# A decoder trunk with a top-2-of-8 mixture of experts: pairs of weight loads split in smaller pieces, and parts of the first expert's and the plan's work moved

## The chip, the cores and the metric

The kernel runs on one core of one Trainium2 chip. The metric is the device time of one execution in microseconds (us), the median of several runs.

## What is computed

Layer 0 is a recurrent mixer beside cross-attention into 256 memory tokens, then a dense SwiGLU. Layer 1 is differential attention beside memory cross-attention, then a mixture of eight SwiGLU experts of which each of the 256 tokens uses two. Every sub-layer ends in a layer norm. All data are fp32. The change touches the experts and the router ahead of them:

```python
logits = (xt @ w_router).astype(jnp.float32)
top_v, top_e = lax.top_k(logits, TOP_K)
gates = jax.nn.softmax(top_v, axis=-1)
...
def expert_block(args):
    xb, e = args
    gu = xb @ w13[e]
    return (jax.nn.silu(gu[:, :EXPERT_DIM]) * gu[:, EXPERT_DIM:]) @ w2[e]
```

D_MODEL is 1024 and EXPERT_DIM 3584, so the experts' weights are 8 x 3 x 1024 x 3584 fp32 numbers, 352 MB, which are read once.

## The kernel before, in words

**Weights.** Each weight is split on the chip into an upper part (fp32r, a copy by ScalarE, L124 or L130) and a lower part (the weight less its upper part, a subtraction by VectorE, L106 or L131), and TensorE multiplies with both. The class `Stream` (L32 to L148) does this for all weights in one fixed order. A load of 1 MB, 128 x 2048 numbers, goes into a free slot: one of four `raw` tiles or `x_hi`, which come back after the split, or, once each, `h3_hi`, `h3_lo` and four `early` tiles `e0` to `e3` (L1032). A split takes places from `room`: five `part` tiles, `h1` (a tile named `h` in the rows) and `x_lo`, each 128 x 2048. All loads are issued by SP, in order; a load waits in SP's queue until the subtraction that read its slot is done. `take` (L135) first calls `split` as far as places are free and then hands out the next pieces; a place comes back with the last piece that it holds.

A load is split in one of three ways. The first stage's two loads (`whole` false) are split by 1024 columns, each piece with both parts in one place: four small sets. All others (`whole` true) are split whole: upper part in one place, lower part in another, two pieces. For the stages of place 1 (`whole` "pair") two loads are split whole one after the other, and their pieces are interleaved only when both are done, because a block of place 1 uses column halves of both loads in turn.

**Places and stages.** The experts stand in places 0 to 7: place 0 is expert 0, the others follow by number of tokens (`PLACE`, L207). Places 2, 3 and 4 have 128 rows, 0 and 5 to 7 have 64, place 1 has 128 + 8. Each place has 21 stages, `g`, `u` and `w` for each of seven blocks of 512 hidden columns, and each stage uses two loads. `moe_seq` (L241 to L248) writes out the order: seven stages of place 0 (`head`), then places 2 and 0 mixed, place 3, then each stage of place 1 among three of places 7, 6 and 5, then place 4. The `g` and `u` stages of place 1 go to `run_moving` (L1347), where the weights stand still and the tokens move (L1365, L1366). The other stages multiply at L368 to L370 (128 rows) or L1276 and L1277 (64 rows).

**The router.** After the last layer norm's first half the loop at L996 transposes each token tile (L1005, copied by ScalarE at L1006), multiplies with the router (L1008) and keeps TensorE busy with other matmuls (`keep_warm`, 6 and 15). VectorE then picks two experts per token (L1039 to L1068), makes the dispatch matrix of expert 0 (`dispatch`, L1086), and `gather_first` (L1216) collects its tokens with TensorE. During the router `st.hold` keeps `split` from making anything.

**The plan.** What the other places need is made by a generator, `plan` (L1099 to L1179): the order of the experts, ranks, dispatch matrices of all places, gates, counts, the two parts `h3_hi` and `h3_lo` of the tokens, and `y`, the tokens scaled. A second generator, `gather(4, True, blocks[2])`, collects the tokens of place 2. Both stand in `slow`; `beat_` (L1210) takes one step of `slow` after each piece of weights during the first stages. Place 2's first stage waits for its gather.

## Time and profile before

| what | value |
|---|---|
| runs | median 1576.31 us of 3 (1575.55 to 1577.61) |
| profiled execution | 1579.21 us |
| its span | 1577.4 us |
| TensorE matmul busy | 1533.0 us (97%) |
| VectorE busy | 1239.3 us (79%) |
| ScalarE busy | 1055.8 us (67%) |
| GpSimd busy | 31.9 us (2%) |
| moved by DMA | 451.60 MB, 286 GB/s mean |

The span runs from the first to the last instruction of the profiled execution. Engines are PE (TensorE matmul), PEld (its weight load), DVE (VectorE), ACT (ScalarE), POOL (GpSimd) and SP, whose queue (SPq) issues the loads. Busy shares are means over stages with different limits, so the rows below are taken stage by stage. The experts run from about 574 us to the end.

### The profile page before, as it was taken

What the parts mean: (1) busy time and instruction counts of PE and PEld (TensorE: products, weight loads), DVE (VectorE), ACT (ScalarE), POOL (GpSimd) and SP (SyncE); (2) the same over time, 40 slices, a digit from 0 to 9 for tenths busy, and PEclk for the clock granted to TensorE, in tenths of its full rate; (3) what the DMA queues carried; (4) which work ended last, traced back from release to release, by engine and by line L of the source; (5) the groups of instructions that cost most, each with busy time, mean ns of one, the idle gap of its engine ahead of it and who ended that gap; (6) DMA issues with size and microseconds to landing.
All of it is one profiled execution on the core that took longest, in us unless ns stands there. A gap on an engine that the chain in (4) does not pass through costs nothing.

```text
span 1577.4 us, 22581 instructions
## 1 busy us (share of the span) xinstructions
PE 1533.0 (97%) x8697; PEld 1300.5 (82%) x8697; DVE 1239.3 (79%) x1205; ACT 1055.8 (67%) x1142; POOL 31.9 (2%) x60
## 2 busy tenths in 40 slices
PE   8999999999999989999999999999999999999996
PEld 7988999999998857887888888887878787877774
DVE  6678654555757579888999879889899899889876
ACT  5784544444456457877887778778778787877663
POOL 0000000000000111000000000000000000000000
PEclk9999999999999999999999999999999999999998
DMA  9454655555533755999999999999999999999982
GB/s 295 161 187 161 233 183 183 183 182 197 167 128 126 265 206 194 377 377 387 395 389 352 333 324 353 356 377 377 357 339 377 371 373 353 361 371 363 333 307 98
DMA packets 218678, 451.60 MB, mean 286 GB/s; under 512 B 7241, under 2 KB 62610, under 8 KB 218562
## 3 DMA queue, kind: packets, MB, share of 16 engines
q1 hardware_dynamic: 217490, 446.76, 79.2%
q0 software_dynamic: 1072, 3.32, 0.7%
q8 instruction: 70, 1.15, 0.3%
q14 instruction: 46, 0.38, 0.1%
HBM read 449.00 MB, written 1.05 MB: 285 GB/s over the span
## 4 chain that ended last, share of the span: by engine, by line
PE 79%; DVE 10%; ACT 4%; DMA 4%; issue 2%; POOL 0%; POOLq 0%; SPq 0%; DVEq 0%; ACTq 0%
PE mm L368 11%; PE mm L370 11%; PE mm L369 11%; PE acc L369 6%; PE acc L370 6%; PE acc L368 6%; DVE part L106 5%; PE mm L1276 4%; PE mm L1277 4%; PE mm L1365 3%; DMA raw<-in_moe_w 3%; PE acc L1277 3%; PE acc L1276 3%; PE mm L1299 2%; PE mm L1255 1%
## 5 line engine op out<-in xcount | busy, mean ns | idle before, releaser
L124 ACT ACTIVATE part<-raw 128x2048 fp32r<-128x2048 f32 x188 | 359.2, 1914 | 58.9 <-DMA raw<-in_moe_w 21.6
L106 DVE TENSOR_TENSOR part<-raw,part 128x2048 fp32r<-128x2048 f32 x150 | 341.1, 2284 | 16.1 <-PE mm L370 5.5
L131 DVE TENSOR_TENSOR part<-raw,part 128x1024 fp32r<-128x1024 f32 x166 | 201.4, 1223 | 126.2 <-ACT part L130 125.6
L130 ACT ACTIVATE part<-raw 128x1024 fp32r<-128x1024 f32 x166 | 173.1, 1056 | 87.8 <-PE mm L370 47.8
L368 PE MATMUL mm<-x_hi,part 128*128 128x256 f32 x768 | 220.0, 286 | 2.1 <-ACT part L130 2.1
L370 PE MATMUL mm<-x_hi,part 128*128 128x256 f32 x768 | 218.3, 284 | 1.1 <-DVE part L131 1.1
L369 PE MATMUL mm<-x_lo,part 128*128 128x256 f32 x768 | 217.7, 283 | 0.0
L368 PEld LDWEIGHTS mm<-x_hi,part 128*128 128x128 f32 x768 | 147.9, 193 | 5.3 <-ACT part L130 2.6
L370 PEld LDWEIGHTS mm<-x_hi,part 128*128 128x128 f32 x768 | 147.8, 192 | 1.7 <-DVE part L131 1.6
L369 PEld LDWEIGHTS mm<-x_lo,part 128*128 128x128 f32 x768 | 147.8, 192 | 0.7
L1276 PE MATMUL mm<-part,xs 128*128 128x512 f32 x248 | 98.8, 398 | 0.0
L124 ACT ACTIVATE part<-x_hi 128x2048 fp32r<-128x2048 f32 x46 | 88.0, 1914 | 15.2 <-PE mm L1277 4.0
L1277 PE MATMUL mm<-part,xs 128*128 128x512 f32 x248 | 97.9, 395 | 0.0
L368 PE MATMUL mm<-part,xg 128*128 128x512 f32 x240 | 97.1, 404 | 0.0
L369 PE MATMUL mm<-part,xg 128*128 128x512 f32 x240 | 95.2, 397 | 1.8 <-DVE part L106 1.5
L370 PE MATMUL mm<-part,xg 128*128 128x512 f32 x240 | 94.7, 395 | 0.0
L106 DVE TENSOR_TENSOR part<-x_hi,part 128x2048 fp32r<-128x2048 f32 x37 | 84.5, 2285 | 7.5 <-PE mm L1365 2.5
L106 DVE TENSOR_TENSOR x_lo<-raw,h 128x2048 fp32r<-128x2048 f32 x37 | 84.6, 2285 | 5.8 <-PE mm L370 2.8
L106 DVE TENSOR_TENSOR h<-raw,part 128x2048 fp32r<-128x2048 f32 x38 | 86.8, 2284 | 1.6 <-ACT part L124 1.1
L106 DVE TENSOR_TENSOR part<-raw,x_lo 128x2048 fp32r<-128x2048 f32 x37 | 84.5, 2285 | 2.7 <-PE mm L1365 1.1
L124 ACT ACTIVATE x_lo<-raw 128x2048 fp32r<-128x2048 f32 x37 | 70.8, 1914 | 13.9 <-PE mm L1277 5.1
L1365 PE MATMUL mm<-xg,part 128*128 128x272 f32 x320 | 79.6, 335 | 0.0
(513 smaller groups left out, 3489.5 us busy)
## 6 DMA issues: line engine op xcount, KB each, us to landing
raw<-in_moe_w SPq DMA_DIRECT2D x262, 1024.0 KB, 7.3
x_hi<-in_moe_w SPq DMA_DIRECT2D x66, 1024.0 KB, 7.3
raw<-in_ffn_w SPq DMA_DIRECT2D x42, 1024.0 KB, 4.9
raw<-in_a_w_in SPq DMA_DIRECT2D x10, 1024.0 KB, 9.4
raw<-in_mem_w_kv SPq DMA_DIRECT2D x8, 1024.0 KB
raw<-in_w_kv_shared SPq DMA_DIRECT2D x8, 1024.0 KB, 6.1
raw<-in_a_w_out SPq DMA_DIRECT2D x6, 1024.0 KB, 4.8
raw<-in_b_w_q SPq DMA_DIRECT2D x6, 1024.0 KB
```

Of the source, the lines that this page charges most:

```text
L106: nc.vector.tensor_sub(lo, src, hi.bitcast(F32))
L124: nc.scalar.activation(hi, src, AF.Copy)
L130: nc.scalar.activation(hi, src, AF.Copy)
L131: nc.vector.tensor_sub(lo, src, hi.bitcast(F32))
L368: PE.matmul(o, lhsT=l_hi, rhs=r_hi, start=start, stop=False)
L369: PE.matmul(o, lhsT=l_hi, rhs=r_lo, start=False, stop=False)
L370: PE.matmul(o, lhsT=l_lo, rhs=r_hi, start=False, stop=stop)
L1255: PE.matmul(p[:, k], lhsT=src[:, t, f], rhs=disp[:, t, g0:g0 + ng], start=t == 0, stop=t == 1)
L1276: PE.matmul(o[h], lhsT=w[:, kt], rhs=w_hi[:, i, f], start=a, stop=False)
L1277: PE.matmul(o[h], lhsT=w[:, kt], rhs=w_lo[:, i, f], start=False, stop=z)
L1299: PE.matmul(p[:, i], lhsT=src[:, i * 128:(i + 1) * 128], rhs=fold, start=True, stop=True)
L1365: PE.matmul(p[m], lhsT=w_hi[:, k, f], rhs=x_[:, kt], start=a, stop=False)
```

## The change

1. A pair of place 1 is split by 1024 columns: `piece` hands out the first half of the first load, the first of the second, the second of the first and the second of the second, and each takes one place for both parts.
2. The last three of the first stage's four small sets are made during the router: `upper` makes the upper parts between the two token tiles, `lower` the lower parts at three points of VectorE's work.
3. In `plan` the dispatch of place 2 comes first, then the two parts of the tokens, as soon as the loads in those two tiles have been split (`uses(once)`), then the gather of place 2, and only then the dispatches of the other places.

```diff
@@ -42,7 +42,7 @@
 
         self.nc, self.free, self.room = nc, deque(free), deque(room)
         self.todo, self.loaded, self.ready, self.hold = deque(), deque(), deque(), False
-        self.known, self.half, self.pair = False, None, None
+        self.known, self.half, self.turn, self.uppers = False, None, 0, deque()
 
     def add(self, ap, a, b, cols=False, whole=False):
 
@@ -65,7 +65,7 @@
             pool, name, again = slot
             v = pool.tile([128, 2048], F32, name=name)[:, :a * b].rearrange("p (a b) -> p a b", a=a)
             self.nc.sync.dma_start(v, ap() if callable(ap) else ap)
-            self.loaded.append(([v] if whole else self.halves(v, cols), cols, whole, slot))
+            self.loaded.append(([v] if whole is True else self.halves(v, cols), cols, whole, slot))
 
     @staticmethod
     def halves(v, cols):
@@ -85,7 +85,7 @@
     def uses(self, slots):
 
         return any(slot in slots for slot in list(self.free) + [l[3] for l in self.loaded] +
-                   ([self.half[3]] if self.half else []))
+                   ([self.half[3]] if self.half else []) + [u[3] for u in self.uppers])
 
     def tiles(self, place, n, m, parts):
         pool, names, _ = place
@@ -94,41 +94,75 @@
         t = pool.tile([128, 2048], F32R, name=names[0])[:, :parts * n * m]
         return t.rearrange("p (s a b) -> s p a b", s=parts, a=n)
 
+    def piece(self):
+
+        todo, cols, whole, slot = self.loaded[0]
+        if whole == "pair":
+
+            if len(self.loaded) < 2:
+                return None
+            second = self.loaded[1]
+            first, self.turn = self.turn == 0, 1 - self.turn
+            if first:
+                src = todo.pop(0)
+                return src, cols, whole, None if todo else slot
+            src = second[0].pop(0)
+            if second[0]:
+                return src, cols, whole, None
+            self.loaded.popleft()
+            self.loaded.popleft()
+            return src, cols, whole, second[3]
+        src = todo.pop(0)
+        if not todo:
+            self.loaded.popleft()
+        return src, cols, whole, None if todo else slot
+
+    def upper(self):
+
+        src, _, whole, slot = self.piece()
+        assert whole is False
+        place = self.room.popleft()
+        hi, lo = self.tiles(place, *src.shape[1:], 2)
+        self.nc.scalar.activation(hi, src, AF.Copy)
+        self.uppers.append((hi, lo, src, slot, place))
+
+    def lower(self):
+
+        hi, lo, src, slot, place = self.uppers.popleft()
+        self.nc.vector.tensor_sub(lo, src, hi.bitcast(F32))
+        if slot:
+            self.back(slot)
+        self.ready.append((hi, lo, (place,)))
+
     def split(self):
         nc = self.nc
         self.load()
         while self.room and not self.hold and (self.loaded or self.half):
-            place = self.room.popleft()
             if self.half:
-                hi, src, cols, slot, first, whole = self.half
+                hi, src, cols, slot, first = self.half
                 self.half = None
+                place = self.room.popleft()
                 lo = self.tiles(place, *src.shape[1:], 1)[0]
                 nc.vector.tensor_sub(lo, src, hi.bitcast(F32))
                 self.back(slot)
                 pieces = list(zip(self.halves(hi, cols), self.halves(lo, cols)))
-                pieces = [(*w, (first, place) if w is pieces[-1] else ()) for w in pieces]
-                if whole == "pair" and not self.pair:
-                    self.pair = pieces
-                else:
-                    if self.pair:
-                        pieces = [w for two in zip(self.pair, pieces) for w in two]
-                        self.pair = None
-                    self.ready += pieces
+                self.ready += [(*w, (first, place) if w is pieces[-1] else ()) for w in pieces]
             else:
-                todo, cols, whole, slot = self.loaded[0]
-                src = todo.pop(0)
-                if not todo:
-                    self.loaded.popleft()
-                if whole:
+                got = self.piece()
+                if not got:
+                    break
+                src, cols, whole, slot = got
+                place = self.room.popleft()
+                if whole is True:
                     hi = self.tiles(place, *src.shape[1:], 1)[0]
                     nc.scalar.activation(hi, src, AF.Copy)
-                    self.half = hi, src, cols, slot, place, whole
+                    self.half = hi, src, cols, slot, place
                 else:
-                    if not todo:
-                        self.back(slot)
                     hi, lo = self.tiles(place, *src.shape[1:], 2)
                     nc.scalar.activation(hi, src, AF.Copy)
                     nc.vector.tensor_sub(lo, src, hi.bitcast(F32))
+                    if slot:
+                        self.back(slot)
                     self.ready.append((hi, lo, (place,)))
             self.load()
 
@@ -993,7 +1027,8 @@
             ln_tail(*ahead[0], gb, h3[:, 0])
     l1t.close()
     hp = ctx.enter_context(tc.tile_pool(name="hp", bufs=1, side="right"))
-    st.free += [(hp, "h3_hi", False), (hp, "h3_lo", False)]
+    once = [(hp, "h3_hi", False), (hp, "h3_lo", False)]
+    st.free += once
     st.load()
 
     hT = lp.tile([128, 2, KT, 128], F32, name="vd")
@@ -1009,6 +1044,10 @@
         keep_warm((6, 15)[t])
         if t:
             ln_tail(*ahead[1], gb, h3[:, 1])
+            st.lower()
+        else:
+            for _ in range(3):
+                st.upper()
     l1.close()
     catp.close()
     pa.close()
@@ -1065,6 +1104,7 @@
         PE.matmul(ct[:, 16:24], lhsT=ones, rhs=mb[:, t], start=t == 0, stop=t == 1)
     val = S("val", 2, 8)
     DVE.tensor_scalar(val, mb, -BIG, BIG, op0=OP.mult, op1=OP.add)
+    st.lower()
     DVE.tensor_add(val, val, ct[:, :16].rearrange("p (t e) -> p t e", t=2))
     rank = S("rank", 2, 8)
     gate = S("gate", 2, 8)
@@ -1087,6 +1127,7 @@
                               op0=OP.is_equal)
 
     dispatch((0, 0, 64), val)
+    st.lower()
 
     ord_i = mo.tile([1, NE - 1], I32, name="ord_i")
     cs_i = mo.tile([1, NE + 1], I32, name="cs_i")
@@ -1130,12 +1171,22 @@
             POOL.tensor_tensor(tmp[:, t], sel, val[:, t, None, 1:].to_broadcast([128, q, q]), op=OP.mult)
         DVE.tensor_reduce(rank[:, :, 1:], tmp, axis=AX.X, op=OP.add)
         yield
+        dispatch(*PLACE[2])
+        yield
+        while st.uses(once):
+            yield
+        h3_parts.extend(hp.tile([128, 2, D], F32R, name=f"h3_{s}") for s in ("hi", "lo"))
+        hi, lo = h3_parts
+        for t in range(2):
+            ACT.activation(hi[:, t], h3[:, t], AF.Copy)
+            DVE.tensor_sub(lo[:, t], h3[:, t], hi[:, t].bitcast(F32))
+            yield
+        yield from gather(4, True, blocks[2])
         for bs in PLACE.values():
             for b in bs:
-                if b[0]:
+                if b[0] not in (0, 2):
                     dispatch(b)
-            if bs[0][0] % 2:
-                yield
+                    yield
         g1 = S("g1", 2)
         POOL.tensor_scalar(g1, d, 1.0, None, op0=OP.add)
         DVE.reciprocal(g1, g1)
@@ -1168,12 +1219,6 @@
         POOL.tensor_copy(cs_i[:, :NE], cs[0:1])
         POOL.tensor_copy(cs_i[:, NE:], over[0:1])
         yield
-        h3_parts.extend(hp.tile([128, 2, D], F32R, name=f"h3_{s}") for s in ("hi", "lo"))
-        hi, lo = h3_parts
-        for t in range(2):
-            ACT.activation(hi[:, t], h3[:, t], AF.Copy)
-            DVE.tensor_sub(lo[:, t], h3[:, t], hi[:, t].bitcast(F32))
-            yield
         for t in range(2):
             ACT.activation(y[:, t], h3[:, t], AF.Copy, scale=ALPHA)
             yield
@@ -1500,7 +1545,7 @@
         (4, "g", 3): [late_gb],
         (4, "u", NJ - 1): [wait_slow, lambda: setattr(last, "dt", back(last, mt(), F32, "sh", 2))],
     }
-    slow += [plan(), gather(4, True, blocks[2])]
+    slow.append(plan())
     run_experts(moe_seq, blocks, st, hooks)
     wait_slow()
 
```

On VectorE around the router's end (names of tiles as in the rows; `part` and `x_hi`, `x_lo` are the places and slots above), before:

```order
L1067 TENSOR_SCALAR val<-mb 128x16
L1068 TENSOR_TENSOR val<-val,mm 128x16
L1086 TENSOR_SCALAR disp<-slots,val 128x64 x2
L1228 TENSOR_TENSOR ys_5466<-mm,ys_5466 128x2x64 x2
L1228 TENSOR_TENSOR ys_5466<-mm,ys_5466 128x4x64
L131 TENSOR_TENSOR part_5492<-x_hi,part_5492 128x1024
L131 TENSOR_TENSOR part_5497<-x_lo,part_5497 128x1024
L131 TENSOR_TENSOR part_5500<-x_lo,part_5500 128x1024
L106 TENSOR_TENSOR h_5505<-raw_5095,part_5503 128x2048
L106 TENSOR_TENSOR part_5519<-raw_5152,x_lo 128x2048
```

and now:

```order
L465 SCALAR_TENSOR_TENSOR h_5058<-qd,rstd,kd 128x512 x2
L132 TENSOR_TENSOR part_5367<-x_hi,part_5367 128x1024
L1078 SCALAR_TENSOR_TENSOR lg<-mm,rstd,b_rt 128x8 x2
...
L1106 TENSOR_SCALAR val<-mb 128x16
L132 TENSOR_TENSOR part_5369<-x_lo,part_5369 128x1024
L1108 TENSOR_TENSOR val<-val,mm 128x16
L1126 TENSOR_SCALAR disp<-slots,val 128x64 x2
L132 TENSOR_TENSOR part_5371<-x_lo,part_5371 128x1024
L1273 TENSOR_TENSOR ys_5477<-mm,ys_5477 128x2x64 x2
L1273 TENSOR_TENSOR ys_5477<-mm,ys_5477 128x4x64
L146 TENSOR_TENSOR h_5505<-raw_5095,part_5503 128x2048
L146 TENSOR_TENSOR part_5519<-raw_5152,x_lo 128x2048
```

The three subtractions of 128 x 1024 that stood behind the gather's (`ys`) now stand ahead of the router's first step (`lg`), ahead of `val` and behind the dispatch of expert 0.

On VectorE between the ranks and the split of place 2's first set, before (a `disp` row with 128 columns is a whole place, with 64 a place of 64 rows):

```order
L1131 TENSOR_REDUCE rank<-tmp 128x2x7
L1086 TENSOR_SCALAR disp<-slots,rank 128x128 x2
...
L106 TENSOR_TENSOR part_5584<-raw_5234,part_5562 128x2048
L1086 TENSOR_SCALAR disp<-slots,rank 128x64 x6
L106 TENSOR_TENSOR x_lo<-h_hi,h_5588 128x2048
L1086 TENSOR_SCALAR disp<-slots,rank 128x128 x6
L1141 RECIPROCAL g_5632<-g_5632 128x2
L106 TENSOR_TENSOR part_5636<-h_lo,part_5609 128x2048
...
L106 TENSOR_TENSOR part_5775<-x_hi,part_5743 128x2048
L106 TENSOR_TENSOR x_lo<-raw_5507,h_5779 128x2048
L106 TENSOR_TENSOR part_5830<-raw_5555,part_5805 128x2048
L106 TENSOR_TENSOR part_5856<-raw_5560,part_5834 128x2048
```

and now:

```order
L1172 TENSOR_REDUCE rank<-tmp 128x2x7
L1126 TENSOR_SCALAR disp<-slots,rank 128x128 x2
L146 TENSOR_TENSOR part_5578<-raw_5234,part_5562 128x2048
L146 TENSOR_TENSOR x_lo<-h_hi,h_5582 128x2048
L146 TENSOR_TENSOR part_5614<-h_lo,part_5597 128x2048
...
L146 TENSOR_TENSOR x_lo<-raw_5507,h_5765 128x2048
L1126 TENSOR_SCALAR disp<-slots,rank 128x64 x4
L146 TENSOR_TENSOR part_5808<-raw_5555,part_5787 128x2048
L1126 TENSOR_SCALAR disp<-slots,rank 128x64 x2
L1126 TENSOR_SCALAR disp<-slots,rank 128x128 x2
L146 TENSOR_TENSOR part_5826<-raw_5560,part_5812 128x2048
L1126 TENSOR_SCALAR disp<-slots,rank 128x128 x2
```

Of the dispatches only that of place 2 stays ahead of the splits of the first stages; four of 128 columns, two of 64 and the plan's later steps now stand behind the split of place 2's first set (`part_5808<-raw_5555`, before `part_5856<-raw_5560` and `part_5830<-raw_5555`).

On VectorE at the first stage of place 1 (L1372, now L1417, is the stage's first tail), before:

```order
L1435 TENSOR_TENSOR sg<-sg,mm 128x512
L106 TENSOR_TENSOR part_8229<-raw_8082,part_8206 128x2048
L106 TENSOR_TENSOR x_lo<-raw_8120,h_8233 128x2048
L1308 TENSOR_TENSOR hd<-mm,hd 128x512
L106 TENSOR_TENSOR part_8276<-raw_8146,part_8251 128x2048
L1372 TENSOR_TENSOR sg<-sg,mm 128x136 x2
L106 TENSOR_TENSOR part_8337<-x_hi,part_8280 128x2048
L1372 TENSOR_TENSOR sg<-sg,mm 128x136 x2
L106 TENSOR_TENSOR h_8365<-raw_8204,part_8341 128x2048
```

and now:

```order
L163 TENSOR_TENSOR part_8206<-raw_8082,part_8206 128x1024
L1480 TENSOR_TENSOR sg<-sg,mm 128x512
L163 TENSOR_TENSOR part_8230<-raw_8120,part_8230 128x1024
L163 TENSOR_TENSOR h_8233<-raw_8082,h_8233 128x1024
L163 TENSOR_TENSOR x_lo<-raw_8120,x_lo 128x1024
L1353 TENSOR_TENSOR hd<-mm,hd 128x512
L146 TENSOR_TENSOR part_8280<-raw_8146,part_8255 128x2048
L146 TENSOR_TENSOR part_8302<-x_hi,part_8284 128x2048
L1417 TENSOR_TENSOR sg<-sg,mm 128x136 x2
L146 TENSOR_TENSOR h_8347<-raw_8204,part_8329 128x2048
L1417 TENSOR_TENSOR sg<-sg,mm 128x136 x2
```

The pair (`raw_8082` and `raw_8120`) was two whole subtractions and is four small ones in order of use, and at the first tail one more whole set has been split.

On SP the order of the loads changes in one place: the second load into `x_hi` comes ahead of the four into the early tiles instead of behind them.

## Rows read from the trace of the kernel before

**Rows 1.** Busy time by stretch: start:end, length, PE, PEld, DVE, ACT, POOL, clock, DMA share, GB/s
```profile
575.00:622.00 47.00, 38.65 (x172) 29.34 (x173) 43.29 (x56) 39.58 (x40) 10.78 (x25) 0.93 0.48 169
622.00:675.00 53.00, 53.00 (x267) 44.15 (x266) 45.30 (x28) 41.98 (x40) 0.00 (x0) 1.00 1.02 373
957.00:1406.00 449.00, 435.16 (x2444) 365.44 (x2443) 402.55 (x319) 353.29 (x346) 0.64 (x1) 1.00 1.00 364
991.00:995.00 4.00, 4.00 (x22) 3.96 (x22) 3.31 (x3) 2.11 (x3) 0.00 (x0) 0.57 0.90 355
```

**Rows 2.** Timeline of ACT, 561 to 580 us: start, us, instruction, idle before and releaser
```profile
561.90 1.09 ACT L1006 ACTIVATE vd<-mm 128x512 f32<-128x512 f32 x2 [3.30 <-PE mm L1005]
574.28 1.05 ACT L130 ACTIVATE part<-x_hi 128x1024 fp32r<-128x1024 f32 x1
575.23 2.00 ACT L130 ACTIVATE part<-x_lo 128x1024 fp32r<-128x1024 f32 x2
577.13 1.91 ACT L124 ACTIVATE part<-raw 128x2048 fp32r<-128x2048 f32 x1
```

**Rows 3.** Timeline of DVE, 564 to 582 us
```profile
564.54 0.36 DVE L1039 SCALAR_TENSOR_TENSOR lg<-mm,rstd,b_rt 128x8 f32<-128x8 f32 x2 [1.83 <-PE mm L1008]
569.59 0.17 DVE L1068 TENSOR_TENSOR val<-val,mm 128x16 f32<-128x16 f32 x1 [2.00 <-PE mm L1065]
576.51 2.35 DVE L131 TENSOR_TENSOR part<-x_lo,part 128x1024 fp32r<-128x1024 f32 x2
579.07 2.29 DVE L106 TENSOR_TENSOR h<-raw,part 128x2048 fp32r<-128x2048 f32 x1 [0.20 <-ACT part L124]
```

**Rows 4.** The page's costliest groups: busy, mean ns of one, idle before and releaser
```profile
L124 ACT ACTIVATE part<-raw 128x2048 fp32r<-128x2048 f32 x188 | 359.2, 1914 | 58.9 <-DMA raw<-in_moe_w 21.6
L106 DVE TENSOR_TENSOR part<-raw,part 128x2048 fp32r<-128x2048 f32 x150 | 341.1, 2284 | 16.1 <-PE mm L370 5.5
L131 DVE TENSOR_TENSOR part<-raw,part 128x1024 fp32r<-128x1024 f32 x166 | 201.4, 1223 | 126.2 <-ACT part L130 125.6
L130 ACT ACTIVATE part<-raw 128x1024 fp32r<-128x1024 f32 x166 | 173.1, 1056 | 87.8 <-PE mm L370 47.8
```

**Rows 5.** Timeline of SP's queue, 560 to 630 us
```profile
564.58 2.78 SPq L67 DMA_DIRECT2D e<-in_moe_w  x4
615.85 0.37 SPq L67 DMA_DIRECT2D x_hi<-in_moe_w  x1
617.95 7.46 SPq L67 DMA_DIRECT2D raw<-in_moe_w  x4
```

**Rows 6.** Timeline of DVE, 591 to 621 us
```profile
591.75 1.06 DVE L1086 TENSOR_SCALAR disp<-slots,rank 128x64 fp32r<-128x64 f32 x6
594.93 1.25 DVE L1086 TENSOR_SCALAR disp<-slots,rank 128x128 fp32r<-128x128 f32 x6
596.11 0.15 DVE L1141 RECIPROCAL g<-g 128x2 f32<-128x2 f32 x1
605.45 0.16 DVE L1167 TENSOR_SCALAR cs<-cs 128x8 f32<-128x8 f32 x1
617.84 2.28 DVE L106 TENSOR_TENSOR part<-raw,part 128x2048 fp32r<-128x2048 f32 x1
```

**Rows 7.** Timeline of PE, 621.9 to 623 us
```profile
622.01 0.39 PE L368 MATMUL mm<-part,xg 128*128 128x512 f32 x1
```

**Rows 8.** Timeline of DVE, 1088 to 1096 us, in the stretch of place 1
```profile
1091.35 4.49 DVE L106 TENSOR_TENSOR part<-raw,part 128x2048 fp32r<-128x2048 f32 x2
```

**Rows 9.** Who waited for whom, 957 to 1406 us: total, times, longest
```profile
DVE part L106 <- PE mm L1365: 6.1, 5, 1.2
PE acc L1277 <- DVE part L106: 4.8, 5, 1.3
ACT part L124 <- PE mm L1366: 3.8, 5, 0.9
```

**Rows 10.** DMA issues, 957 to 1406 us: count, KB each, median us to landing
```profile
raw<-in_moe_w SPq DMA_DIRECT2D x124, 1024.0 KB, 7.2
```

## The prediction, before the changed kernel was timed

> **What bounds the kernel now.** I read the table of stretches first, then the timelines of ScalarE (ACT), VectorE (DVE), TensorE (PE) and the SP queue around the start of the experts, then who waited for whom in the stretch of place 1. The table [rows 1] shows three kinds of time. From 575 to 622 us, the first seven stages of expert 0, DVE is busy 43.29 of 47 us, PE 38.65, and the transfers only 0.48 of the time: the splits set the pace. From 622 to 675 PE is full (53.00 of 53) and the transfers are too (1.02, 373 GB/s). From 957 to 1406, where place 1 runs between narrow stages, PE is busy 435.16 of 449 us, DVE 402.55, and the transfers move 364 GB/s: no engine is far from full, and 13.84 us of PE's time is idle. What a change can win is thus bounded by two idle times of PE: 47 - 38.65 = 8.35 us at the start and 13.84 us in the stretch of place 1.
>
> **Three small sets split during the router.** Before, ACT makes its first three small upper parts of expert 0 at 574.28 and 575.23 (1.05 and 2.00 us), and only then, at 577.13, that of the first whole set [rows 2]. DVE makes the matching lower parts until 578.86 and begins on the whole set at 579.07 [rows 3]. These three copies and three subtractions move into the router. The copies go ahead of ACT's read of the second token tile at 561.90, before which ACT idles 3.30 us [rows 2]; three of them take 3 x 1.056 = 3.17 us [rows 4], so they just fit. The first subtraction goes where DVE idles 1.83 us before 564.54, the second where it idles 2.00 us before 569.59 [rows 3]; each is 1.22 us [rows 4], so both fit. The third stands behind the dispatch of expert 0, where DVE waits for the gather's copies; if that cover is short, its 1.22 us comes off what follows. After the gather ACT begins at once on the whole set: 577.13 - 574.28 = 2.85 us earlier, and DVE with it.
>
> On SP the second load of x_hi now stands ahead of the four into the early tiles. It waits for DVE's first small subtraction, which ends by 564.54 - 1.83 + 1.22 = 563.93. The four issued at 564.58 before [rows 5], so the moved load fits in front and pushes them by about one issue, half a us at most. Nothing waits for them for 25 us.
>
> **The plan of place 2 ahead.** DVE runs without a real pause from 579.07 to the split of place 2's first set at 617.84 [rows 3, 6]. Among its work are dispatches that the first stages do not need. In the new order these stand behind that split: two of 64 columns, 2 x 0.18 (1.06 for six) = 0.35 us; four of 128 columns, 4 x 0.21 (1.25 for six) = 0.83 us; and six small plan steps, the first at 596.11 and the last at 605.45, of 0.15 to 0.26 us, about 1.07 us together [rows 6]. The rest of the dispatches still stand ahead of it, and so gain nothing at that point. Sum: 2.85 + 0.35 + 0.83 + 1.07 = 5.1 us by which DVE reaches place 2's first set earlier. The moved work comes back, on a DVE that is busy 45.30 of 53 us while PE is full [rows 1], so I cost it at nothing; without that cover it is 2.25 us.
>
> PE began place 2 at 622.01 [rows 7] and should now begin at about 615 to 617. It does not idle for 53 us after that, so its shift lasts if the transfers come earlier too. They do: the load into x_hi at 615.85, the first after the gap, and the four from 617.95 wait for DVE's splits of those slots [rows 5]. The x_hi tile is now loaded one place earlier, so its next split stands four whole subtractions earlier on DVE (4 x 2.2 us) besides the 5.1, and one load of five moves into the idle gap. The next loads follow DVE by about 5. **I take -5 us**; the ends are -2.85 (the dispatches come back in full, and only the small sets count) and -8.35 (all of PE's idle time there).
>
> **Place 1's pairs by 1024 columns.** Before, a pair's two loads were split whole, one after the other, into four tiles of parts, and no piece could be used until the fourth was written; two tiles came back only behind the third piece. Now each piece is copied and subtracted alone, in order of use, in one tile that comes back behind it. There are 14 such stages, 28 loads.
>
> What it adds: 28 subtractions and 28 copies. By single durations a set costs DVE 2 x 1.223 - 2.284 = 0.162 us more and ACT 2 x 1.056 - 1.914 = 0.198 [rows 4], or 4.5 and 5.5 us. Back to back less shows: two small subtractions take 2.35 us from start to end [rows 3], so they start 1.13 apart; two whole ones take 4.49 [rows 8], so 2.21 apart; the difference is 2 x 1.13 - 2.21 = 0.05 us a set, 1.4 us in all. Both stand beside PE's work.
>
> What it removes: DVE waited 6.1 us, and ACT 3.8, for place 1's matmuls to give a tile back [rows 9]. PE idled 13.84 us in the stretch [rows 1], the largest part at the narrow stages just behind place 1 (4.8 us at one line) [rows 9], where DVE had fallen behind; one stall also left the clock at 1.2 GHz for part of 991 to 995 (0.57 mean) [rows 1]. In the new order DVE stands one whole set (2.2 us) further on when place 1's first tail comes. No stall of the commonest kind is longer than 1.3 us [rows 9], so a set in hand covers it; but DVE at 402.55 of 449 and transfers at 364 of 373 GB/s leave little, and another stall may follow. DVE's net is 6.1 - 1.4 = 4.7, or 6.1 - 4.5 = 1.6 by single durations. The transfers' room is 449 x (1 - 364/373) = 10.8 us. **I take -5 us**, nearest to the back-to-back price because DVE is rarely idle there. The ends are +4.5 (only the added time counts) and -10.8.
>
> Here the row and a rule differ in size. The Trainium skill (VectorE: DVE Perf Modes, The TRN2 errata) says that an operation pays a fixed extra cost per instruction, so that many small tiles pay it each time. It speaks against this part; read as the difference of single durations it would take away nearly all of the -5, and it is the third rival.
>
> **The sum.** The profiled execution took 1579.2 us (span 1577.4, 1.8 around it); -5 - 5 gives 1569.2. That execution was 2.9 us above the median of the three runs, 1576.3, so I forecast **1566.3 us**, with a range of its own of 1561 to 1570.
>
> **The rivals** (times on the median's scale; about 0.2%, 3 us, is what a measurement here can tell).
> 1. Only the start pays. For it: DVE and the transfers are nearly full in the stretch of place 1, so a stall removed may come back at the next stage. Against: DVE's wait for tiles is a cost that the change takes away directly. 1576.3 - 5 = 1571.3.
> 2. Both pay in full: PE's idle time goes at both places, 8.35 and, as far as the transfers allow, 10.8. For it: PE is otherwise full. Against: the splits at the start still take longer than PE's work there. 1576.3 - 19 = 1557.
> 3. The finer pieces cost their fixed part. For it: 0.162 us a set on DVE, the busiest engine but PE; 4.5 us would come off the start's 5. Against: the back-to-back rows show 0.05. About 1575.8: no difference. By the skill's rule named above it would come out here; the trace agrees that there is a fixed part, but most of it is hidden between neighbours.
> 4. Slower: late slots. The first raw tile of a pair was free after one subtraction of 2.28 us; now after three small ones, 3 x 1.13 to 3 x 1.22, so 1.1 to 1.4 us later, and SP issues in order, so every load behind it is late too. 14 pairs x 1.4 = 19.6 us if nothing hides it. A load takes 7.2 us from issue to landing [rows 10], so two or more are on their way, which hides one late issue; it decides where fewer than one is queued. If half shows, +9.8 - 5 = +4.8: 1581. Against: the copies can now start with one tile free instead of two, which gives much of it back.
>
> **How the numbers follow.** Forecast 0.52, rival one 0.22, rival two 0.09, rival three 0.10, rival four 0.07. The range of 1557 to 1574 takes in the forecast and rivals one and two; rivals three and four, 0.17 together, lie outside. Faster by over 0.2% (below 1573.2) 0.83, within 0.2% 0.10, slower 0.07.
>
> **What would show it.** Right: the whole set's first subtraction starts near 576.3 instead of 579.07; the first load after the gap near 600 instead of 615.85, and the four behind it near 613; PE's first matmul of place 2 near 616 instead of 622.01; the same stage 5 us ahead at the start of place 1, and about 10 at the end; DVE's 6.1 us for place 1's matmuls gone; PE's 13.84 us of idle time down to about 9. Wrong: the small copies delay ACT's read at 561.90 and the whole router with it; PE's lead at 622 is gone by 750, the transfers then being the limit; or the SP queue shows gaps behind each pair.

## The result: slower, 1622.3 us, and the profile after

The change made the kernel slower by 45 us. The median is 1622.28 us against 1576.96 in the same comparison, a ratio of 1.0285 with a 95% interval of 1.0265 to 1.0306. One of the four executions behind this median took 2125.7 us at a mean granted clock of 0.65, and the ratio is of the other three. The forecast was 1566.3 us, with a range of 1557 to 1574, so the result lies 48 us beyond the range's slow end and on the other side of no change. The profiled execution took 1622.2 us, its span 1620.2.

**The start did what was expected.** These are ScalarE (ACT) and VectorE (DVE) of the changed kernel around the router's end, where the small sets went: start, us, instruction, idle before and releaser.

```profile
558.36 2.00 ACT L126 ACTIVATE part<-x_lo 128x1024 fp32r<-128x1024 f32 x2
560.83 1.09 ACT L1041 ACTIVATE vd<-mm 128x512 f32<-128x512 f32 x2 [0.47 <-PE mm L1040]
573.21 1.91 ACT L158 ACTIVATE part<-raw 128x2048 fp32r<-128x2048 f32 x1
```

```profile
563.47 0.36 DVE L1078 SCALAR_TENSOR_TENSOR lg<-mm,rstd,b_rt 128x8 f32<-128x8 f32 x2 [0.70 <-PE mm L1043]
568.51 0.17 DVE L1108 TENSOR_TENSOR val<-val,mm 128x16 f32<-128x16 f32 x1 [0.85 <-PE mm L1104]
575.15 2.29 DVE L146 TENSOR_TENSOR h<-raw,part 128x2048 fp32r<-128x2048 f32 x1 [1.38 <-ACT part L158]
612.16 0.74 DVE L1126 TENSOR_SCALAR disp<-slots,rank 128x64 fp32r<-128x64 f32 x4
612.81 2.29 DVE L146 TENSOR_TENSOR part<-raw,part 128x2048 fp32r<-128x2048 f32 x1
```

The three copies fit ahead of the read of the second token tile: ACT still waits 0.47 us for it, and it starts at 560.83 instead of 561.90 [rows 2]. The two subtractions fill the idle time ahead of `lg` and `val`, 1.83 and 2.00 us before [rows 3], 0.70 and 0.85 now. The first whole set's subtraction starts at 575.15 instead of 579.07 [rows 3]. About 1.1 of these 3.9 us were there before the router's end already (the reads of `vd` and `lg` are 1.07 us earlier), so about 2.85 remain for the small sets, which is the forecast's term. The rest of the start follows in SP's queue and on TensorE (PE):

```profile
562.79 0.37 SPq L67 DMA_DIRECT2D x_hi<-in_moe_w  x1
563.56 3.71 SPq L67 DMA_DIRECT2D e<-in_moe_w  x4
596.65 0.37 SPq L67 DMA_DIRECT2D x_hi<-in_moe_w  x1
612.28 8.75 SPq L67 DMA_DIRECT2D raw<-in_moe_w  x4
```

```profile
614.04 0.39 PE L402 MATMUL mm<-part,xg 128*128 128x512 f32 x1
615.16 0.50 PE L403 MATMUL mm<-part,xg 128*128 128x512 f32 x1 [0.73 <-DVE part L146]
```

The load into x_hi goes out at 596.65 instead of 615.85 and the four behind it from 612.28 instead of 617.95 [rows 5]; PE begins place 2 at 614.04 instead of 622.01 [rows 7]. Place 1's first matmul with moving tokens comes at 930.1 instead of 937.3 us: until there the kernel is 7.2 us ahead, about 1.1 of them from before the router's end.

**All of the loss lies in place 1's stretch.** From its first to its last such matmul it took 428.5 us (937.3 to 1365.8) and now takes 479.3 (930.1 to 1409.4), 50.8 more; the 7.2 us of the start come off, and the last expert matmul is 42.8 us later. Busy time by stretch, columns as in [rows 1]; first the kernel before in its stretch:

```profile
937.30:1365.80 428.50, 415.93 (x2381) 352.63 (x2380) 383.58 (x304) 338.01 (x336) 0.00 (x0) 1.00 0.99 363
```

and the changed kernel in its own:

```profile
930.10:1409.40 479.30, 438.82 (x2381) 370.52 (x2380) 389.58 (x331) 336.86 (x363) 0.00 (x0) 0.95 0.90 327
```

DVE works 6.0 us more in the stretch (389.58 - 383.58), ACT 1.2 us less. So it is not work that grew, but waiting: PE's idle time rose from 428.5 - 415.93 = 12.6 to 479.3 - 438.82 = 40.5 us, and the same matmuls took 22.9 us longer at a mean granted clock of 0.95 instead of 1.00. Transfers fell from 363 to 327 GB/s.

Who waited for whom in these two stretches (total, times, longest), first before:

```profile
ACT hs L1307 <- DVE sh L1303: 21.2, 15, 2.8
ACT hd L1377 <- DVE sg L1376: 16.6, 13, 2.2
ACT sg L1374 <- DVE sg L1372: 5.3, 14, 0.4
```

and the changed kernel, with its transfers from 957 to 1406 us (count, KB each, us to landing) behind it:

```profile
ACT hs L1352 <- DVE sh L1348: 39.5, 17, 4.2
ACT hd L1422 <- DVE sg L1421: 34.0, 13, 3.5
ACT sg L1419 <- DVE sg L1417: 33.2, 14, 2.4
DVE part L146 <- ACT part L158: 24.2, 21, 2.3
PE acc L1322 <- DVE part L146: 14.7, 11, 1.8
```

```profile
raw<-in_moe_w SPq DMA_DIRECT2D x112, 1024.0 KB, 5.9
```

The wait that I had wanted gone, DVE for place 1's matmuls (6.1 us [rows 9]), is gone. In its place ACT waits for DVE and DVE for ACT. ACT waits for `hd` of place 1's u stages 34.0 against 16.6 us before, for the Silu of its g stages (`sg`) 33.2 against 5.3, and for `hs` of the narrow places 39.5 against 21.2. One u stage, place 1's third, shows how. The two engines in the changed kernel:

```profile
1016.84 1.90 ACT L158 ACTIVATE h<-raw 128x2048 fp32r<-128x2048 f32 x1
1018.65 0.44 ACT L1415 ACTIVATE sg<-mm 128x136 f32<-128x136 f32 x2
1021.99 0.43 ACT L1422 ACTIVATE hd<-sg 128x272 fp32r<-128x272 f32 x1 [2.90 <-DVE sg L1421]
1022.33 1.90 ACT L158 ACTIVATE part<-raw 128x2048 fp32r<-128x2048 f32 x1
```

```profile
1018.78 2.29 DVE L146 TENSOR_TENSOR x_lo<-raw,h 128x2048 fp32r<-128x2048 f32 x1
1020.99 0.50 DVE L1417 TENSOR_TENSOR sg<-sg,mm 128x136 f32<-128x136 f32 x2
1022.46 0.51 DVE L1424 TENSOR_TENSOR hd<-sg,hd 128x256 fp32r<-128x256 f32 x2 [0.50 <-ACT hd L1422]
1024.26 2.29 DVE L146 TENSOR_TENSOR part<-raw,part 128x2048 fp32r<-128x2048 f32 x1 [1.30 <-ACT part L158]
1026.47 0.49 DVE L1417 TENSOR_TENSOR sg<-sg,mm 128x136 f32<-128x136 f32 x2
```

A tail is what stands behind each half of a place 1 stage. In a u stage ACT copies, DVE adds and multiplies, ACT makes `hd` and DVE subtracts; in a g stage ACT copies, DVE adds and ACT takes the Silu. ACT has made `h`, the last upper part, and copied its two halves of the tail by 1019.1; then it stands for 2.90 us, because DVE first subtracts the whole `x_lo` (2.29 us) and only then comes to the tail. While ACT stands it can't make the next upper part, so after the tail DVE stands for 1.30 us in turn. The tails are 1026.47 - 1020.99 = 5.48 us apart. A u stage of the kernel before, place 1's fourth:

```profile
1084.15 0.43 ACT L1377 ACTIVATE hd<-sg 128x272 fp32r<-128x272 f32 x1 [0.87 <-DVE sg L1376]
1084.50 1.92 ACT L124 ACTIVATE x_lo<-raw 128x2048 fp32r<-128x2048 f32 x1
1088.25 0.43 ACT L1377 ACTIVATE hd<-sg 128x272 fp32r<-128x272 f32 x1 [1.50 <-DVE sg L1376]
```

```profile
1083.14 0.50 DVE L1372 TENSOR_TENSOR sg<-sg,mm 128x136 f32<-128x136 f32 x2 [0.48 <-ACT sg L1370]
1085.05 2.28 DVE L106 TENSOR_TENSOR h<-x_hi,part 128x2048 fp32r<-128x2048 f32 x1
1087.25 0.49 DVE L1372 TENSOR_TENSOR sg<-sg,mm 128x136 f32<-128x136 f32 x2
```

There the lower part of the last upper one comes behind the tail (`h`, at 1085.05), so DVE has work in hand as soon as the tail is done, and the tails are 4.11 us apart. Over all seven u stages the two `hd` copies of a stage start 5.65 us apart on average in the changed kernel and 4.46 before. At this 1.2 us for each of their 14 tails the u stages would lose 17 us, an estimate; what each kind of stage loses is tested below.

Counted in the order of the instructions, as upper parts ahead of a tail's first copy on ACT less lower parts ahead of its addition on DVE, it is the same at every tail:

```
upper parts ahead, 28 tails of place 1:   before  1 in 28      changed  0 in 28
```

It flips because of where places come back. Seven places hold the splits. Before, none of a pair's four places had come back by its first tail and two had by its second, so the odd seventh place went to an upper part whose lower part had to wait. Now one place has come back by a pair's first tail and three by its second, so the waiting lower part finds a place, and goes ahead of the tail.

### The profile page after: what moved, and what is told of

Read it like the earlier page. It is cut to its first block, busy times and chain, and to the rows that moved or that the text cites. A ratio compares the mean times of both kernels' runs of the same rounds, so it can differ in the third digit from the quotient of the medians.

```text
span 1620.2 us, 22615 instructions
## 1 busy us (share of the span) xinstructions
PE 1551.7 (96%) x8697; PEld 1317.3 (81%) x8697; DVE 1243.5 (77%) x1233; ACT 1054.3 (65%) x1170; POOL 31.0 (2%) x60
## 3 DMA queue, kind: packets, MB, share of 16 engines
HBM read 449.00 MB, written 1.05 MB: 278 GB/s over the span
## 4 chain that ended last, share of the span: by engine, by line
PE 73%; DVE 10%; ACT 9%; DMA 4%; issue 4%; POOL 0%; DVEq 0%; SPq 0%; POOLq 0%; ACTq 0%
PE mm L402 11%; PE mm L403 10%; PE mm L404 10%; PE acc L403 6%; PE acc L402 6%; PE acc L404 6%; DVE part L146 5%; PE mm L1321 4%; PE mm L1322 4%; ACT part L158 3%; PE acc L1322 2%; PE acc L1321 2%; ACT part L162 2%; PE mm L1344 2%; DMA raw<-in_moe_w 2%
## 5 line engine op out<-in xcount | busy, mean ns | idle before, releaser
L158 ACT ACTIVATE part<-raw 128x2048 fp32r<-128x2048 f32 x171 | 326.1, 1911 | 50.7 <-DMA raw<-in_moe_w 19.1
L163 DVE TENSOR_TENSOR part<-raw,part 128x1024 fp32r<-128x1024 f32 x200 | 242.1, 1223 | 129.3 <-ACT part L162 127.3
L146 DVE TENSOR_TENSOR part<-raw,part 128x2048 fp32r<-128x2048 f32 x136 | 309.9, 2287 | 27.8 <-ACT part L158 19.8
L162 ACT ACTIVATE part<-raw 128x1024 fp32r<-128x1024 f32 x200 | 207.9, 1056 | 88.3 <-PE mm L404 48.7
L1321 PE MATMUL mm<-part,xs 128*128 128x512 f32 x248 | 101.3, 408 | 3.9 <-DVE sg L1417 3.7
L1322 PE MATMUL mm<-part,xs 128*128 128x512 f32 x248 | 100.2, 404 | 0.0
L158 ACT ACTIVATE part<-x_hi 128x2048 fp32r<-128x2048 f32 x43 | 82.3, 1913 | 14.6 <-PE mm L1322 6.1
L146 DVE TENSOR_TENSOR h<-raw,part 128x2048 fp32r<-128x2048 f32 x35 | 80.0, 2287 | 13.1 <-ACT part L158 11.4
L146 DVE TENSOR_TENSOR x_lo<-raw,h 128x2048 fp32r<-128x2048 f32 x34 | 77.8, 2288 | 11.4 <-ACT h L158 7.2
L146 DVE TENSOR_TENSOR part<-raw,x_lo 128x2048 fp32r<-128x2048 f32 x34 | 77.7, 2286 | 8.9 <-ACT x_lo L158 6.8
L158 ACT ACTIVATE x_lo<-raw 128x2048 fp32r<-128x2048 f32 x34 | 65.0, 1911 | 14.3 <-PE mm L1322 6.3
```

The source lines that it names most:

```text
L146: nc.vector.tensor_sub(lo, src, hi.bitcast(F32))
L158: nc.scalar.activation(hi, src, AF.Copy)
L162: nc.scalar.activation(hi, src, AF.Copy)
L163: nc.vector.tensor_sub(lo, src, hi.bitcast(F32))
L1321: PE.matmul(o[h], lhsT=w[:, kt], rhs=w_hi[:, i, f], start=a, stop=False)
L1322: PE.matmul(o[h], lhsT=w[:, kt], rhs=w_lo[:, i, f], start=False, stop=z)
```

## The experiments

Theory A is this order: an upper part must stand ahead of a tail. The rivals are B, the fixed cost of finer splits; C, the raw tiles that come back later; and D, that the plan's moves upset what follows. "Place 1's stretch" is always from its first to its last moving matmul.

### The start alone, and the pairs alone

The start alone keeps the pairs whole; the pairs alone keep the router and the plan of before. Cut to the lines that decide, against the changed kernel, the start alone and then the pairs alone:

```diff
-            self.loaded.append(([v] if whole is True else self.halves(v, cols), cols, whole, slot))
+            self.loaded.append(([v] if whole else self.halves(v, cols), cols, whole, slot))
...
-                if whole is True:
+                if whole:
```

```diff
-            st.lower()
-        else:
-            for _ in range(3):
-                st.upper()
...
-    slow.append(plan())
+    slow += [plan(), gather(4, True, blocks[2])]
```

> The two moves at the start alone, pairs split whole as before. Theory A (the whole loss lies in place 1, where no upper part stands ahead of the tails any more): about 1570 us, as the changed kernel began place 2 at 614.0 instead of 622.0, of which about 1 us came from earlier work. Theory B (fixed cost of smaller splits) and theory C (late raw tiles) expect the same here. Theory D (moving the plan upset the later order): about 1620.

> The pairs by 1024 columns alone, the start as before. Theories A, B and C: slower than the changed kernel by what the start gains, about 1622 + 7 = 1629 us. Theory D: about 1577.

The start alone: 1572.28 us, ratio 0.9972 (0.996 to 0.9984), place 1's stretch 429.2. The pairs alone: 1625.14 us, 1.0305 (1.0289 to 1.0321), place 1's stretch 475.9. The loss is the pairs' alone and the start pays 0.28%, 4.4 us; 4.4 off and 48 on make 44, against the 45 of the whole change. D falls.

### The tail first

The changed kernel, with the split held back at the second and fourth pieces of a place 1 stage, so that nothing new stands ahead of the two tails. Arithmetic, tiles and the number of small sets are the same.

```diff
             for k2 in range(2):
+                s.hold = k2 == 1
                 w_hi, w_lo = s.get()
+                s.hold = False
```

> The changed kernel, but no split is made at the second piece of each half of a place 1 stage, so that the lower part that stood ahead of the tail stands behind it; the splits and their sizes are the same. Theory A: the loss is gone, 1565 to 1573 us. Theory B: still about 1620, the same small operations are there. Theory C: still about 1620, the raw tiles come back no sooner.

1580.07 us, ratio 1.0015 (1.0006 to 1.0024), place 1's stretch 434.9, one upper part ahead at 28 of 28 tails. Order alone gives 42 us back. That is theory A for nearly all of it, though short of the 1565 to 1573 that I had said. Some 8 us to the start alone stay, and B could still claim them: ACT's wait for `sh` at the narrow places is 40.7 us in this stretch, as long as in the changed kernel.

### Place 1's u stages alone, and its g stages alone

The same hold in one kind of stage (here u; the other run says "g"):

```diff
-                s.hold = k2 == 1
+                s.hold = k2 == 1 and kind == "u"
```

> The changed kernel with the tail first in place 1's u stages alone: 14 of its 28 tails have an upper part standing ahead, the 14 of the g stages none. It tells what each kind of tail costs. Theory A, with the loss shared as ScalarE's waits in place 1's stretch grew from before to after (the Silu of g waits for VectorE's addition 33.2 instead of 5.3 us, the copy to hd of u waits for VectorE's product 34.0 instead of 16.6 us): u carries 17.4 of 45.3, so of the 42 us that both bring back about 16, total 1606 us (1600 to 1612), place 1 in about 462 us. If only u's longer way (ScalarE, VectorE, ScalarE, VectorE) matters: 1580 to 1585 us. If a single wait in a pair of stages is enough to lose it all: 1618 to 1622 us.

> The same in place 1's g stages alone, the tails of u as in the changed kernel. Theory A, shared as above: g carries 27.9 of 45.3, so about 26 of the 42 us come back, total 1596 us (1590 to 1602), place 1 in about 452 us; and the two runs' gains add up to that of both (42 us), within 6 us. If only u matters: 1618 to 1622 us.

u alone: 1603.74 us, place 1 in 463.0 us; g alone: 1594.84 us, in 449.2. Both totals came out within 2.5 us of theory A's numbers, which were worked out from the growth of ACT's two waits, and the gains, 18.5 and 27.4 us, add up to 45.9 against 42.2 for both. ACT's waits, first with the tail first in u:

```profile
ACT sg L1421 <- DVE sg L1419: 33.2, 14, 2.4
ACT hd L1424 <- DVE sg L1423: 15.7, 13, 2.2
```

and with the tail first in g:

```profile
ACT hd L1424 <- DVE sg L1423: 36.6, 13, 3.5
ACT sg L1421 <- DVE sg L1419: 5.4, 14, 0.4
```

Each edit took away its own wait (`hd` of u, the Silu `sg` of g) and left the other about as in the changed kernel.

### Four part tiles instead of five, in both kernels

With six places in place of seven the order turns around: the changed kernel then has one upper part ahead at all 28 tails, and the kernel before has none.

```diff
-N_PARTS = 5
+N_PARTS = 4
```

> The changed kernel with four part tiles instead of five. One place less turns the count of free places, so that an upper part stands ahead of every tail again. Theory A: faster than the changed kernel in spite of the smaller buffer, 1575 to 1605 us. Theories B and C: slower than the changed kernel, over 1622, since it has less to work ahead with.

> The kernel before (pairs split whole) with four part tiles instead of five, so six places in place of seven. The order of the two engines then has no upper part standing ahead of the lower parts at any of the 28 tails of place 1, where before had one at every tail. It is the counterpart of the changed kernel with four part tiles (1652.6 us, place 1 in 465.7 us, one upper ahead). Theory A (what counts is whether an upper part stands ahead of place 1's tails, not how a pair is split): place 1's stretch 490 to 530 us, against 428.5 before and 465.7 in the counterpart, and the total 1665 to 1710 us. Theory B (the small splits cost by themselves) and theory C (late slots): without them this kernel must be faster than the counterpart, place 1 in 430 to 465 us, total 1605 to 1650 us.

The changed kernel with four: 1652.63 us, ratio 1.0468 (1.0451 to 1.0485). My 1575 to 1605 missed it. Its place 1 took 465.7 us, 13.6 less than with five part tiles, but place 1 began 34.6 us later (964.7 against 930.1): the lost place costs elsewhere. At the other places the order turned the other way: the 21 tails of the wide places' hidden columns had one upper part ahead at `hd` and have none with four, and of the narrow places' 28, counted at `hs`, 16 had one and none has. That this is the cause outside place 1 was not tried by itself.

The kernel before with four: 1746.98 us, 1.1082 (1.1066 to 1.1099), place 1 in 551.9 us. It is slower than its counterpart by 94 us, without a finer pair in it, where B and C expected it faster. The wide and the narrow places have lost their upper part in both of these kernels, so in the order the two differ mainly at place 1's tails. Busy time in its stretch and who waited for whom there:

```profile
967.00:1518.90 551.90, 469.72 (x2381) 387.63 (x2379) 388.37 (x304) 338.40 (x336) 0.00 (x0) 0.91 0.80 283
```

```profile
DVE part L106 <- ACT part L124: 76.8, 48, 3.9
ACT hs L1307 <- DVE sh L1303: 47.9, 18, 3.2
```

The sign is theory A's, the size is not: I had said 490 to 530 for the stretch and 1665 to 1710 in all. Whole pairs also hold their places longer, which may cost more with six; how the 86 us between the two stretches divide into order and places stays open.

### One upper part always ahead, with fine pairs and with whole ones

The strongest form of theory A: in the experts a lower part is written into the program only after the upper part of the next piece. First the changed kernel with this rule, then the start alone (whole pairs) with it. The same edit, cut to its core:

```diff
+    def later(self, f, slot):
+        self.flush()
+        self.pend = f, slot
+        if not self.ahead:
+            self.flush()
...
                     hi, lo = self.tiles(place, *src.shape[1:], 2)
                     nc.scalar.activation(hi, src, AF.Copy)
-                    nc.vector.tensor_sub(lo, src, hi.bitcast(F32))
-                    if slot:
-                        self.back(slot)
-                    self.ready.append((hi, lo, (place,)))
+                    self.flush()
+
+                    def low(lo=lo, src=src, hi=hi, slot=slot, place=place):
+                        nc.vector.tensor_sub(lo, src, hi.bitcast(F32))
+                        if slot:
+                            self.back(slot)
+                        self.ready.append((hi, lo, (place,)))
+
+                    self.later(low, slot)
...
+    st.ahead = True
```

> The changed kernel, in which, from the first stage of the experts on, a lower part is written into the program only after the upper part of the next piece: so one upper part is always ahead, at the tails of place 1 (28 of 28) and at the other stages' tails too. The same arithmetic, tiles and loads. Theory A: place 1's stretch falls from 479 to 425 to 435 us, the total to 1567 to 1575 us, level with the start alone (1572.3) or a little better, as the remaining 8 us of the run with the tail first were the narrow stages' tails, which it left behind the lower parts. Theory B (small splits cost by themselves): 1577 to 1582 us, no better than the run with the tail first (1580.1). Theory C (raw tiles late): the lower parts now come later and free the slots later, so 1585 us or more.

> The start alone (pairs whole, 1572.3 us) with the same rule of one upper part ahead during the experts. The count at the tails of place 1 stays at one, at the narrow stages' it rises from zero or less to zero or one. Theory A: place 1 already has its upper part ahead, so little is left: 1568 to 1574 us. Against the run with fine pairs and the same rule it tells what splitting the pairs finely is worth by itself: theory B expects this one 5 us or more faster than that one, theory A within 3 us of it, and my prediction's reason (a pair's pieces come sooner) would have this one 3 us or more slower.

Fine pairs: 1572.17 us, ratio 0.9967 (0.9955 to 0.9979). Whole pairs: 1572.94 us, 0.9975 (0.9965 to 0.9985). The small splits are all still there in the first, and the loss is gone, the 8 us that the tail-first run had left included: of the narrow places' 28 tails, counted at the Silu, 13 stood one upper part short of the start alone in that run, and one does now. ACT's waits in the stretch are nearly back where they were before: 16.5 us for `hd`, 5.3 for the Silu, 27.9 for `hs`. Place 1's third u stage again, ACT and DVE with fine pairs and one ahead:

```profile
1007.25 1.92 ACT L176 ACTIVATE h<-raw 128x2048 fp32r<-128x2048 f32 x1
1010.38 0.43 ACT L1450 ACTIVATE hd<-sg 128x272 fp32r<-128x272 f32 x1 [0.87 <-DVE sg L1449]
```

```profile
1009.37 0.50 DVE L1445 TENSOR_TENSOR sg<-sg,mm 128x136 f32<-128x136 f32 x2 [0.34 <-ACT sg L1443]
1011.27 2.29 DVE L162 TENSOR_TENSOR x_lo<-raw,h 128x2048 fp32r<-128x2048 f32 x1
1013.48 0.49 DVE L1445 TENSOR_TENSOR sg<-sg,mm 128x136 f32<-128x136 f32 x2
```

The subtraction that writes `x_lo` has changed sides with the tail, and the tails are 4.11 us apart as before. The stretch, with fine pairs:

```profile
931.60:1359.40 427.80, 414.60 (x2381) 353.42 (x2379) 385.97 (x330) 339.78 (x363) 0.00 (x0) 0.99 0.99 364
```

and with whole pairs:

```profile
930.70:1358.20 427.50, 414.53 (x2382) 351.12 (x2379) 383.86 (x304) 337.45 (x336) 0.00 (x0) 1.00 1.00 364
```

427.8 and 427.5 us: once the order is right, the finer pairs are worth nothing in either direction. C falls as well, since the lower parts, and with them the return of the raw tiles, stand later in the program here than in the changed kernel. These two and the start alone beat both kernels, by a quarter to a third of a per cent, and their intervals overlap; the start alone is the simplest of them.

### The small sets without the plan

The start alone, with the plan in its old order:

```diff
-        yield from gather(4, True, blocks[2])
...
-    slow.append(plan())
+    slow += [plan(), gather(4, True, blocks[2])]
```

> The kernel before with the three small sets of expert 0 split during the router and nothing else: pairs whole, the plan in its old order. The two moves at the start together gave 1572.3 against 1577.0 (ratio 0.9972). The prediction's steps give 2.85 us to the small sets and 2.25 us to the plan: this run then stands 2 to 3 us below before, ratio 0.998 to 0.999, PE's first matmul of place 2 near 619. If the small sets carry the whole gain: 1571 to 1573 and place 2 near 617. If they carry none (the moved load, or the plan, did it): 1576 to 1578.

1574.2 us, ratio 0.999 (0.9979 to 1.0). PE begins place 2 at 618.1 us, against 622.0 before and 617.0 with both moves. Place 1 begins at 932.6 us, against 932.5 with both. The time agrees with the 2.85 us forecast for the small sets: 2.5 us between the medians, 0 to 3.3 by the interval. What the plan adds is less certain. The start alone's 617.0 and 932.5 come from an execution 2.9 us above its median; the six other profiles with both moves and seven places (the changed kernel, the tail first in both or either kind of stage, one ahead with fine and with whole pairs) begin place 2 at 614.0 to 615.5 us and place 1 at 930.0 to 931.6. Against these the plan brings 2.6 to 4.1 us at place 2's begin and 1.0 to 2.7 at place 1's. In the total it is 1.9 us between two medians whose ratios' intervals overlap.

## Why the prediction was wrong

**The step that failed** is this one: "In the new order DVE stands one whole set (2.2 us) further on when place 1's first tail comes. No stall of the commonest kind is longer than 1.3 us [rows 9], so a set in hand covers it". The order rows were read rightly, one more whole subtraction stands ahead of the first tail. But it was read as a set in hand. I had asked what DVE gains by being ahead, and not who waits for the tail that this set now precedes: ACT does, 2.90 us at a time in the stage shown, and ACT's next upper part is queued behind that wait, and DVE's next subtraction behind that part. The prediction followed what is queued behind a wait on SP, and not on ACT. It had also read place 1's stretch as "no engine is far from full", though ACT is busy only 353.29 of 449 us there [rows 1]. The term came out at +48 us (the pairs alone) where I had -5, with bounds of +4.5 and -10.8. The bounds were sums of durations and of idle times; neither holds a wait that the new order creates.

The Trainium skill (PSUM — Partial Sum Buffer, Engine vs sequencer instructions) states that the queues of ScalarE and VectorE are strict FIFO. The trace agrees: ACT's copy at 1022.33, for which the trace shows no wait of its own, stood behind the 2.90 us of `hd`. Had I carried that through both queues, it would have spoken against this part.

**Even without that harm the -5 was not there.** DVE's wait for place 1's matmuls is gone in the run with fine pairs and one ahead, and PE's idle time in the stretch is 427.8 - 414.6 = 13.2 us, as with whole pairs (13.0) and before (12.6). What I took away was DVE's idle time, and PE was not waiting for it.

**The start was right.** -5 was forecast, -4.4 measured by itself (0.9972; the interval, -6.3 to -2.5 us). Of its two terms the small sets' 2.85 shows in the trace at the first whole set and agrees with the time of the run that has them alone. The plan's 2.25 shows at place 2's begin; how much of it is left at the end the two runs can't tell.

**The price of a small set was about right.** DVE is busy 385.97 us with fine pairs and 383.86 with whole ones, 2.1 us for 28 sets or 0.08 a set, between the 0.05 read back to back and the 0.162 of single durations. The Trainium skill's rule on many small tiles (VectorE: DVE Perf Modes, The TRN2 errata) names a real cost, which the trace shows at half the size of single durations, and hidden beside PE. Rival three is out.

**The rival on the slow side named the wrong mechanism.** With late slots ACT would have waited for loads. In place 1's stretch of the changed kernel its only wait for a load is 0.6 us; before, these waits made 7.3 us. Loads landed sooner, 5.9 us against 7.2 [rows 10], while transfers ran at 327 instead of 363 GB/s in the two stretches. By these numbers about 1.8 loads of 1 MB were under way at once instead of 2.5, an estimate; that this is why they landed sooner was not tried.

## What to carry to other kernels

Where two in-order engines hand work back and forth, the number of first halves that stand ahead of each exchange is a quantity of its own: count it in the program order, at every place where they meet, before and after a change. Here it went from one to zero through nothing but how many tiles had come back by then, and cost 42 us, while the busy times of the two engines hardly moved. A piece of work that is moved ahead of an exchange is only a lead if nobody waits for the exchange.

## What the runs showed of the hardware

Nearly half of the loss was TensorE's clock. Short waits came close together, and the granted clock fell to its lower level for some six microseconds. The changed kernel by stretches of 2 us:

```profile
1104.00:1106.00 2.00, 0.34 (x1) 0.03 (x1) 2.00 (x1) 2.00 (x3) 0.00 (x0) 1.00 0.50 199
1106.00:1108.00 2.00, 1.83 (x6) 1.54 (x6) 2.00 (x2) 2.00 (x3) 0.00 (x0) 0.52 0.32 56
1108.00:1110.00 2.00, 2.00 (x9) 1.90 (x9) 2.00 (x2) 1.95 (x2) 0.00 (x0) 0.50 1.03 386
1110.00:1112.00 2.00, 2.00 (x6) 1.52 (x6) 1.52 (x4) 1.10 (x2) 0.00 (x0) 0.50 1.05 394
1112.00:1114.00 2.00, 2.00 (x9) 1.59 (x8) 2.00 (x2) 1.23 (x1) 0.00 (x0) 0.77 1.09 376
1114.00:1116.00 2.00, 2.00 (x10) 1.63 (x9) 2.00 (x1) 2.00 (x2) 0.00 (x0) 1.00 1.00 377
```

PE had waited 1.05 us ahead of 1100.69, 0.41 ahead of 1103.85 and 1.83 ahead of 1106.17; then the clock stood at 0.50, 1.2 GHz, and was back at 1.00 by 1114. In the trace's clock records it fell so nine times in this stretch, 48 us in all; before, once, and with fine pairs and one ahead twice. Over the stretch the same 2381 matmuls took 438.82 instead of 415.93 us. So 27.9 us of added idle time brought 22.9 us of slower matmuls with it, and where the waits went, as with one upper part ahead, the matmul time was back at 414.60.
